# RWKV7 key norm as one reciprocal, third-order root steps, free PSUM in the order of work, both heads in 128 rows

## The chip, the cores and the metric

The kernel runs on one core of a Trainium2 chip. The metric is device time in microseconds (us), the median of several executions. Beside the times there is one profiled execution, whose trace is what all rows below come from.

## The reference

Two blocks run one after the other on 512 tokens of 2048 channels: a block with two attention layers, and a block that mixes an RWKV7 branch (16 heads of 64) with an HGRN2 branch (8 heads of 128). The change lies in the second block. What matters of the RWKV7 branch:

```python
kk = _heads(k * k_k, RWKV_HEAD)
kk = kk / jnp.maximum(jnp.sqrt(jnp.sum(kk * kk, -1, keepdims=True)), 1e-12)
k = k * (1.0 + (a - 1.0) * k_a)
o = _rwkv7_scan(rh, _heads(decay, RWKV_HEAD), kh, vh, -kk, kk * ah)
...
sa = jnp.einsum('bhij,bhj->bhi', S, a_t)
S = S * w_t[:, :, None, :] + sa[..., None] * b_t[:, :, None, :] + v_t[..., None] * k_t[:, :, None, :]
```

The normed key enters the state only as the pair `a_t = -kk` and `b_t = kk * a`, and only their product counts. The output of each head is then normed over its 64 channels, by the inverse root of a variance. The HGRN2 branch norms its heads in the same way.

## The kernel before

All large products are tiled as 128x128 weights by 512 tokens. Weights come from HBM in pieces of 128x512, are split into a high and a low part in fp32r (ScalarE writes `wh`, GpSimd writes `wl`), and each product is made of three matmuls: high by high, high by low, low by high. In the trace these are the `proj` matmuls.

The program runs the layers in order: the two attention layers, then the eight RWKV units (two heads each, so 128 channels), then the eight HGRN units, then the output product and a layer norm. Each unit has four column blocks of 48 `proj` matmuls (`mix_groups`). The rest of a unit's work is cut into steps that belong to threads: `rwkv_unit` makes the threads `prep` (decay, key norm, operands), `M` (pair matrices, triangular inverse, the recurrence over four chunks, the head norm), `K` and `B`.

The order of all instructions is fixed while the program is built. A `Clock` (L30) keeps a modelled time of each engine and of each tile. Between two triples of `proj` matmuls, `stream` calls `side` (L341), which goes through the threads and issues each thread's next step if `ready` (L337) says that the modelled results of the step before it, and the events it needs, lie in the past. A step that is needed before something else can go on is issued by `require` (L327), ready or not. Each engine then executes its own instructions strictly in that order, so that a step whose data or PSUM buffer is late holds up whatever stands behind it on the engine.

PSUM is held as four tags: `proj` with three buffers, `s` with two, `t` with two, `y` with one. `ps` (L227) takes the next buffer of a tag. In the modelled time the first write to it then waits until the buffer's last reader is done, but `ready` does not ask for that.

Steps that the change touches: `p_kk2` and `p_kk3` (L1318, L1325) sum the squares of the key per head and norm the key `kq`, with an inverse root by Ln and Exp on ScalarE and one Newton step (`newton_rsqrt`, L478) on VectorE; `m_ar` (L1395) scales the normed key, with a sign, by the decay; `m_split`, `m_split2` and `m_step` (L1402 to L1428) make, chunk by chunk, high and low parts of the operands `bk` and `ar` and from them the pair matrices, in two `s` buffers, one for each head; `small_rsqrt` (L487) is the inverse root of 128x8 or 128x4 numbers on VectorE, from an integer guess and three Newton steps, in `f_2` (L1671) and `fin2` (L1990). Other steps that the prediction names: `p_tok` (L1380) transposes an operand through a `t` buffer, `inv_8` (L1476) is 14 small VectorE instructions, `block_u` and `ch_u` (L1589, L1596) are the recurrence, `m_zo` (L1446) follows `m_step`, and `f_3` transposes the normed heads.

Nearly all instructions stand under one line in the trace, L175, the helper through which they are issued; they are told apart by their tiles.

Of the kernel before, what the change touches and what calls it, by code (L numbers as in the profile page):

```python
# [6 lines left out]
F32 = mybir.dt.float32  # L7
F32R = mybir.dt.float32r
U32 = mybir.dt.uint32
I32 = mybir.dt.int32  # L10
AF = mybir.ActivationFunctionType
ALU = mybir.AluOpType
# [17 lines left out]
class Clock:  # L30
# [7 lines left out]
    def __init__(self):  # L38
        self.t = dict.fromkeys(("tensor", "vector", "scalar", "gpsimd", "sync"), 0.0)
        self.w, self.r, self.free, self.dead = {}, {}, {}, set()  # L40
        self.fin = 0.0
        self.aset = None
        self.mode = None

        self.port = {"vector": [], "gpsimd": []}
# [11 lines left out]
    def note(self, eng, cost, outs, ins, lat=0.0, mode=None, shared=False):  # L57
        t = self.t[eng]
        lat += self.LAT[eng]
        use = {}  # L60
        for aps, kind in ((ins, 0), (outs, 1)):
            for ap in aps:
                name = ap.tensor.name
                assert name not in self.dead, name
                t = max(t, self.free.get(name, 0.0) if kind else 0.0)
                for c in self.cells(ap):
                    use[c] = max(kind, use.get(c, 0))
        for c, kind in use.items():
            f, e = self.w.get(c, (0.0, eng))
            if e != eng or eng != "tensor":  # L70
                t = max(t, f + self.HOP)
            if kind:
                f, e = self.r.get(c, (0.0, eng))
                t = max(t, f + self.HOP if e != eng else 0.0)
        if mode:
            if self.mode not in (None, mode):
                t += self.SWITCH
            self.mode = mode
        if shared:
            for s, f in self.port["gpsimd" if eng == "vector" else "vector"]:  # L80
                if s <= t < f:
                    t = f
            p = self.port[eng]
            p.append((t, t + cost))
            del p[:-24]
        self.t[eng] = t + cost
        fin = t + cost + lat
        for c, kind in use.items():
            d = self.w if kind else self.r
            if d.get(c, (0.0, eng))[0] <= fin:  # L90
                d[c] = (fin, eng)
        self.fin = max(self.fin, fin)

    def last(self, name):

        return max([v[0] for d in (self.w, self.r) for k, v in d.items() if k[0] == name] + [0.0])


def isap(x):
# [89 lines left out]
class Timed:  # L189
    def __init__(self, clock, nc):  # L190
        for n in ("tensor", "vector", "scalar", "gpsimd", "sync"):
            setattr(self, n, Engine(clock, getattr(nc, n), n))


class Kern:
# [29 lines left out]
    P = tmp  # L225
# [58 lines left out]
    def mm(self, out, lhsT, rhs, start, stop, **kw):  # L284
        self.nc.tensor.matmul(out, lhsT, rhs, start=start, stop=stop, **kw)
# [19 lines left out]
    def set(self, ev):  # L305
        self.ev[ev] = self.clock.fin
# [29 lines left out]

    def ready(self, th):  # L337
        return th["steps"] and th["ready"] <= self.clk and all(
            self.ev.get(e, 1e9) <= self.clk for e in th["steps"][0][1])

    def side(self):  # L341
        t0 = self.clk
# [126 lines left out]
        self.thread([(lambda: None, [("acc", layer)], None), (a,), (b, [], ("rsb", layer))],  # L469
                    carry=True)  # L470

    def rsqrt(self, m, r):

        nc = self.nc
        nc.scalar.activation(r, m, AF.Ln, scale=2.0 ** 16)
        nc.scalar.activation(r, r, AF.Exp, scale=-0.5, bias=self.l2c)

    def newton_rsqrt(self, r, m, t):  # L478

        nc = self.nc  # L480
        nc.vector.tensor_tensor(out=t, in0=r, in1=r, op=ALU.mult)
        nc.vector.scalar_tensor_tensor(out=t, in0=t, scalar=-0.5, in1=m, op0=ALU.mult,
                                       op1=ALU.mult)
        nc.vector.scalar_tensor_tensor(out=r, in0=t, scalar=1.5, in1=r, op0=ALU.add,
                                       op1=ALU.mult)

    def small_rsqrt(self, r, m, t):  # L487

        nc = self.nc
        nc.vector.tensor_scalar(r.bitcast(U32), m.bitcast(U32), 1, None, ALU.logical_shift_right)  # L490
        nc.vector.tensor_scalar(r.bitcast(I32), r.bitcast(I32), -1.0, float(0x5f3759df), ALU.mult,
                                ALU.add)
        for _ in range(3):
            self.newton_rsqrt(r, m, t)

    def silu_gate(self, ps, sg):

# [58 lines left out]
    def start(self):  # L556
        nc, I, const = self.nc, self.I, self.const
# [24 lines left out]
        load_x(1)  # L582
        self.ones = self.tile(self.cp, (128, 128), F32, "ones")
        nc.vector.memset(self.ones, 1.0)
        self.l2c = self.tile(self.cp, (128, 1), F32, "l2c")
        nc.vector.memset(self.l2c, 8.0 * float(np.log(2.0)))
        self.rsb = self.tile(self.cp, (128, T), F32, "rsb")
        self.load_raw(2)
        load_x(2)
# [669 lines left out]
    def rwkv_unit(self, st, u):  # L1259
        nc = self.nc  # L1260
        mm, mm3, tr, ps, P = self.mm, self.mm3, self.tr, self.ps, self.P
        c2 = {k: (v[:, u:u + 1]) for k, v in self.c2.items() if k not in ("mu", "omu")}
        S = {}
        sgt, kt, ly, mat = self.sgt, self.kt, self.ly, self.mat[u % 2]
        c4 = lambda t: t.rearrange("p (c t) -> p c t", c=4)
# [52 lines left out]
        def p_kk2():  # L1318
            p = head_sum(S["hi"], S["lo"])
            S["m"], S["rn"] = P("pm", (128, 516)), P("pr", (128, 516))  # L1320
            m, rn = S["m"][:, 0:512], S["rn"][:, 0:512]
            nc.vector.tensor_scalar(m, p, 1e-24, None, ALU.max)
            self.rsqrt(m, rn)

        def p_kk3():  # L1325
            m, rn = S["m"][:, 0:512], S["rn"][:, 0:512]
            self.newton_rsqrt(rn, m, S["sq"])
            nc.gpsimd.tensor_tensor(out=S["kq"], in0=S["kq"], in1=rn, op=ALU.mult)

        def p_dec():  # L1330
            S["cs"] = cs = P("pm", (128, 4, 129))
# [61 lines left out]
        own = [slice(0, 64), slice(64, 128)]  # L1393

        def m_ar():  # L1395
            S["ar"] = ar = P(f"ar{u % 2}", (128, 4, 2, 128))
            nc.vector.scalar_tensor_tensor(out=ar[:, :, 0, :], in0=c4(S["kq"]), scalar=-1.0,
                                           in1=S["P"][:, :, 0:128], op0=ALU.mult, op1=ALU.mult)
            nc.vector.tensor_tensor(out=ar[:, :, 1, :], in0=c4(st["r", u]),
                                    in1=S["P"][:, :, 1:129], op=ALU.mult)  # L1400

        def m_split(c):  # L1402
            def f():
                if c == 0:
                    S["zo"] = P("zo", (128, 4, 2, 128), bufs=2)
                bk = S["bk"][:, c]
                S["bkh", c] = x = P("bkhl", (128, 2, 2, 128), F32R, 2)
                S["arh", c] = y = P("arhl", (128, 3, 2, 128), F32R, 2)
                for h in range(2):
                    nc.scalar.activation(x[own[h], h], bk[own[h]], AF.Copy)  # L1410
                nc.scalar.activation(y[:, 2], S["ar"][:, c], AF.Copy)
            return f

        def m_split2(c):
            def f():
                ar, bk, x, y = S["ar"][:, c], S["bk"][:, c], S["bkh", c], S["arh", c]
                for h in range(2):
                    a, b = own[h], own[1 - h]
                    nc.scalar.activation(y[b, h], ar[a], AF.Copy)
                    nc.vector.tensor_tensor(out=x[b, h], in0=bk[a], in1=x[a, h].bitcast(F32),  # L1420
                                            op=ALU.subtract)
                    nc.vector.tensor_tensor(out=y[a, h], in0=ar[a], in1=y[a, 2].bitcast(F32),
                                            op=ALU.subtract)
            return f

        def m_step(c):  # L1428
            def f():
                p = [ps("s", (128, 2, 256)) for h in range(2)]  # L1430
                x = S["bkh", c]
                y = [S["arh", c][:, i].rearrange("p a t -> p (a t)") for i in range(3)]
                for i in range(2):
                    for h in range(2):
                        mm(p[h][:, i, :], x[own[h], h, i, :], y[2][own[h], :], i == 0, False,
                           skip_group_check=True)
                for h in range(2):
                    for i in range(2):
                        mm(p[h][:, i, :], x[:, h, i, :], y[h], False, i == 1, skip_group_check=True)
                for h in range(2):  # L1440
                    nc.vector.copy_predicated(out=kt[:, h, :], mask=self.mmask, data=p[h][:, 1, :])
                    nc.vector.copy_predicated(out=mat[:, 2 * c + h, :], mask=self.mmask,
                                              data=p[h][:, 0, :])
            return f
# [196 lines left out]
        def ch_o(c):  # L1641
# [17 lines left out]
            out=o.rearrange("p (c h) -> p c h", h=2), in_=v8(i), axis=mybir.AxisListType.X,  # L1659
            op=ALU.add)  # L1660
# [682 lines left out]
```

## Time and profile before

| what | value |
|---|---|
| three runs, us | 3031.47, 3031.53, 3036.08 |
| median, us | 3031.53 |
| profiled execution, time, us | 3026.69 |
| its span from first to last instruction, us | 3024.9 |
| TensorE busy | 2942.7 us, 97% of the span |
| VectorE, ScalarE, GpSimd busy | 52%, 43%, 45% |
| mean granted TensorE clock | 0.985 |

A busy TensorE is not one at its peak: matmuls overlap, and their ends are modelled. A granted clock of 1.00 is 2.4 GHz, one of 0.50 is 1.2 GHz.

### The profile page before, as it was taken

The numbers are of one execution on the slowest core, as the hardware profiler recorded it, in microseconds if no ns is written. First come the engines' busy times: TensorE is split into PE (matmuls) and PEld (weight loads), VectorE is DVE, ScalarE is ACT, GpSimd is POOL, SyncE is SP. The second block draws the span as 40 slices with busy tenths as digits, with TensorE's granted clock in tenths as the row PEclk, the third lists the DMA queues.
The fourth block names the chain that finished last, engine by engine and source line by source line (L and its number), as shares of the span: only waits on it lengthen the run. The fifth ranks groups of instructions, "written<-read, shape, count | busy, mean of one in ns | idle before, by whom it ended". The sixth has DMA issues, their size and how long they took to land. (4 is left out here: it accounts for less than half of the span.)

```text
span 3024.9 us, 47964 instructions
## 1 busy us (share of the span) xinstructions
PE 2942.7 (97%) x17904; PEld 2356.2 (78%) x17904; DVE 1560.2 (52%) x3481; ACT 1302.4 (43%) x2571; POOL 1351.4 (45%) x1105
## 2 busy tenths in 40 slices
PE   8999999999999999999999999999999999999996
PEld 5788888888888888888888876677677787888785
DVE  6433333343431235555531277767777766766436
ACT  6444444444433344444443364444444445545233
POOL 3444444444446543444445652223333344444575
PEclk9999999999999999999999999999989999999998
DMA  4333333333335432222234422222222222222343
GB/s 139 108 87 88 94 91 88 94 91 89 93 91 161 140 94 77 75 79 79 76 121 145 123 81 71 62 65 62 64 69 66 76 68 73 81 77 77 103 120 107
DMA packets 192088, 275.79 MB, mean 91 GB/s; under 512 B 50576, under 2 KB 65872, under 8 KB 191856
## 3 DMA queue, kind: packets, MB, share of 16 engines
q1 hardware_dynamic: 191856, 272.73, 31.6%
q8 instruction: 141, 2.31, 0.3%
q14 instruction: 91, 0.75, 0.1%
HBM read 254.51 MB, written 18.16 MB: 90 GB/s over the span
## 5 line engine op out<-in xcount | busy, mean ns | idle before, releaser
L175 POOL TENSOR_TENSOR wl<-raw,wh 128x512 fp32r<-128x512 f32 x847 | 1123.2, 1328 | 1606.8 <-ACT wh L175 1552.6
L175 PE MATMUL proj<-hh,wh 128*128 128x512 f32 x2624 | 1073.2, 409 | 7.1 <-ACT hh L175 5.9
L175 PE MATMUL proj<-hl,wh 128*128 128x512 f32 x2624 | 1036.7, 395 | 4.5 <-DVE hl L175 4.4
L175 PE MATMUL proj<-hh,wl 128*128 128x512 f32 x2624 | 1037.2, 395 | 3.2 <-POOL wl L175 3.1
L175 ACT ACTIVATE wh<-raw 128x512 fp32r<-128x512 f32 x848 | 530.7, 627 | 822.0 <-PE proj L175 587.1
L175 PEld LDWEIGHTS proj<-hh,wh 128*128 128x128 f32 x2624 | 498.8, 190 | 116.1 <-issue 10.6
L175 PEld LDWEIGHTS proj<-hh,wl 128*128 128x128 f32 x2624 | 499.1, 190 | 114.7 <-POOL wl L175 6.5
L175 PEld LDWEIGHTS proj<-hl,wh 128*128 128x128 f32 x2624 | 500.1, 191 | 95.7 <-DVE hl L175 8.0
L175 PE MATMUL proj<-yh,wh 128*128 128x512 f32 (+1 forms) x640 | 249.8, 390 | 0.0
L175 PE MATMUL proj<-yh,wl 128*128 128x512 f32 (+1 forms) x640 | 248.2, 388 | 0.7 <-POOL wl L175 0.4
L175 ACT ACTIVATE t<-t,sm 128x257 f32<-128x257 f32 (+5 forms) x256 | 133.0, 521 | 257.2 <-DVE sm L175 197.3
L175 PE MATMUL proj<-yl,wh 128*128 128x512 f32 (+1 forms) x632 | 240.9, 388 | 0.0
L175 PEld LDWEIGHTS proj<-yh,wl 128*128 128x128 f32 x640 | 120.2, 188 | 26.8 <-POOL wl L175 2.4
L175 DVE TENSOR_TENSOR pt<-proj,t 128x512 f32<-128x512 f32 x32 | 22.1, 691 | 229.1 <-PE proj L175 116.5
L175 PEld LDWEIGHTS proj<-yh,wh 128*128 128x128 f32 x640 | 120.3, 188 | 24.4 <-issue 0.9
L175 PEld LDWEIGHTS proj<-yl,wh 128*128 128x128 f32 x632 | 118.8, 188 | 23.9 <-issue 0.2
L175 DVE TENSOR_TENSOR qf<-proj,rsb 128x512 f32<-128x512 f32 x48 | 33.2, 691 | 154.5 <-PE proj L175 154.2
L175 DVE TENSOR_SCALAR t<-t,sm 128x256 f32<-128x256 f32 (+3 forms) x256 | 101.7, 418 | 6.7
L175 DVE COPY pt<-t 128x384 f32<-128x384 f32 (+1 forms) x96 | 51.2, 534 | 99.8 <-PE t L175 99.8
L175 DVE RECIPROCAL sm<-sm 128x1 f32<-128x1 f32 (+1 forms) x192 | 31.4, 164 | 117.4 <-ACT t L175 115.8
L175 PE MATMUL t<-ident,t 128*128 128x128 f32 x544 | 90.5, 272 | 0.0
L175 DVE CUSTOM_DVE_ANT_0 t<-s,c 128x128 f32<-128x128 f32 (+2 forms) x128 | 49.9, 390 | 71.6 <-PE s L175 71.6
(412 smaller groups left out, 3752.4 us busy)
## 6 DMA issues: line engine op xcount, KB each, us to landing
raw<-in_w_mix_dram SPq DMA_DIRECT2D x260, 256.0 KB, 3.0
raw<-in_w_fox_dram SPq DMA_DIRECT2D x256, 256.0 KB, 3.0
raw<-in_w_swa_dram SPq DMA_DIRECT2D x144, 256.0 KB, 3.0
raw<-in_w_foxo_dram SPq DMA_DIRECT2D x64, 256.0 KB, 3.2
raw<-in_w_swao_dram SPq DMA_DIRECT2D x64, 256.0 KB, 3.1
raw<-in_w_mixo_dram SPq DMA_DIRECT2D x64, 256.0 KB, 3.1
c<-cd SPq DMA_DIRECT2D x32, 256.0 KB, 3.7
xd<-pt SPq DMA_DIRECT2D x32, 256.0 KB, 2.4
```

The costliest lines, as they stand in the source:

```text
L175: r = f(*a, **k)
```

## The change

There are four edits, all in the second block's part of the program or in the order of its steps.

The key stays as it is, and the key that is taken out (`nk`, a new tile) is the key times the reciprocal of its squared norm: ScalarE's Exp gives the reciprocal at once, one Newton step for a reciprocal takes two VectorE instructions in place of three, and `m_ar`'s first instruction has two operands and no sign.

`small_rsqrt` has one third-order step and one Newton step after the guess, 9 instructions in place of 11.

`ready` asks in addition whether the PSUM buffers that the step takes are free in the modelled time (`banks`, for the steps named in `BANKS`, all of them of the second block).

The high and low parts of `bk` and `ar` keep both heads in 128 rows: two ScalarE and two VectorE instructions of 128 rows for each chunk in place of five and four (three of them of 128 rows). `m_step` then makes twelve matmuls of 64 rows (high by high, high by low, low by high, for two operands and two heads) in place of four of 64 rows and four of 128.

```diff
+BANKS = dict(p_lora="ss", m_step="ss", lev64="s", lev_m="s", **dict.fromkeys(
+    ("p_kk2", "p_bonus", "p_tok", "m_zo", "lev16", "lev16b", "lev32", "lev32b", "ch_z", "ch_u",
+     "ch_u2", "ch_u3", "ch_s", "f_3", "tok", "state", "fin3"), "t"))
 def ready(self, th):
         return th["steps"] and th["ready"] <= self.clk and all(
-            self.ev.get(e, 1e9) <= self.clk for e in th["steps"][0][1])
+            self.ev.get(e, 1e9) <= self.clk for e in th["steps"][0][1]) and self.banks(
+                th["steps"][0][0]) <= self.clk
+    def banks(self, f):
+        name = [n for n in f.__qualname__.split(".") if n not in ("<locals>", "f")][-1]
+        t = 0.0
+        for i, p in enumerate(BANKS.get(name, "")):
+            pool, bufs = self.psum[p]
+            q = self.slots.get((id(pool), p), [])
+            if i >= bufs - len(q):
+                t = max(t, self.clock.last(q[i - (bufs - len(q))]) + self.clock.HOP)
+        return t
...
-    def rsqrt(self, m, r):
+    def rsqrt(self, m, r, n=1):
-        nc.scalar.activation(r, r, AF.Exp, scale=-0.5, bias=self.l2c)
+        nc.scalar.activation(r, r, AF.Exp, scale=-0.5 * n, bias=self.l2c[:, n - 1:n])
...
 def small_rsqrt(self, r, m, t):
-        for _ in range(3):
-            self.newton_rsqrt(r, m, t)
+        nc.vector.tensor_tensor(out=t, in0=r, in1=r, op=ALU.mult)
+        nc.vector.tensor_tensor(out=t, in0=t, in1=m, op=ALU.mult)
+        nc.vector.scalar_tensor_tensor(out=t, in0=t, scalar=-10.0 / 3, in1=t, op0=ALU.add,
+                                       op1=ALU.mult)
+        nc.vector.scalar_tensor_tensor(out=r, in0=t, scalar=5.0, in1=r, op0=ALU.add, op1=ALU.mult)
+        self.newton_rsqrt(r, m, t, 0.375)
...
 def p_kk3():
-            self.newton_rsqrt(rn, m, S["sq"])
-            nc.gpsimd.tensor_tensor(out=S["kq"], in0=S["kq"], in1=rn, op=ALU.mult)
+            nc.vector.tensor_tensor(out=m, in0=m, in1=rn, op=ALU.mult)
+            nc.vector.scalar_tensor_tensor(out=rn, in0=m, scalar=-2.0, in1=rn, op0=ALU.add,
+                                           op1=ALU.mult)
+            S["nk"] = P("nk")
+            nc.gpsimd.tensor_tensor(out=S["nk"], in0=S["kq"], in1=rn, op=ALU.mult)
...
 def m_ar():
-            nc.vector.scalar_tensor_tensor(out=ar[:, :, 0, :], in0=c4(S["kq"]), scalar=-1.0,
-                                           in1=S["P"][:, :, 0:128], op0=ALU.mult, op1=ALU.mult)
+            nc.vector.tensor_tensor(out=ar[:, :, 0, :], in0=c4(S["nk"]), in1=S["P"][:, :, 0:128],
+                                    op=ALU.mult)
...
 def m_split(c):
-                S["bkh", c] = x = P("bkhl", (128, 2, 2, 128), F32R, 2)
-                S["arh", c] = y = P("arhl", (128, 3, 2, 128), F32R, 2)
-                for h in range(2):
-                    nc.scalar.activation(x[own[h], h], bk[own[h]], AF.Copy)
-                nc.scalar.activation(y[:, 2], S["ar"][:, c], AF.Copy)
+                S["x", c] = x = P("bkhl", (128, 2, 2, 128), F32R, 2)
+                S["y", c] = y = P("arhl", (128, 2, 2, 128), F32R, 2)
+                nc.scalar.activation(x[:, 0], S["bk"][:, c], AF.Copy)
+                nc.scalar.activation(y[:, 0], S["ar"][:, c], AF.Copy)
...
 def m_split2(c):
-                for h in range(2):
-                    a, b = own[h], own[1 - h]
-                    nc.scalar.activation(y[b, h], ar[a], AF.Copy)
-                    nc.vector.tensor_tensor(out=x[b, h], in0=bk[a], in1=x[a, h].bitcast(F32),
+                for t, hl in ((S["bk"], S["x", c]), (S["ar"], S["y", c])):
+                    nc.vector.tensor_tensor(out=hl[:, 1], in0=t[:, c], in1=hl[:, 0].bitcast(F32),
                                             op=ALU.subtract)
-                    nc.vector.tensor_tensor(out=y[a, h], in0=ar[a], in1=y[a, 2].bitcast(F32),
-                                            op=ALU.subtract)
...
 def m_step(c):
-                for i in range(2):
-                    for h in range(2):
-                        mm(p[h][:, i, :], x[own[h], h, i, :], y[2][own[h], :], i == 0, False,
-                           skip_group_check=True)
-                for h in range(2):
+                for n, (a, b) in enumerate(((0, 0), (0, 1), (1, 0))):
                     for i in range(2):
-                        mm(p[h][:, i, :], x[:, h, i, :], y[h], False, i == 1, skip_group_check=True)
+                        for h in range(2):
+                            mm(p[h][:, i, :], x[own[h], a, i, :], y[own[h], b, :],
+                               n == i == 0, n == 2 and i == 1, skip_group_check=True)
```

The clock also keeps, in `used`, the last modelled use of each tile, which `last` now returns; the value is the same as before.

## Rows read from the trace of the kernel before

**Rows 1.** Windows: busy of each engine, granted clock; RWKV stage, then HGRN stage.

```profile
core 0: us, PE busy (x) PEld busy (x) DVE busy (x) ACT busy (x) POOL busy (x), PEclk, DMA share, GB/s
1778.00:2405.00 627.00, 587.82 (x4913) 445.71 (x4914) 477.46 (x1016) 276.73 (x540) 200.81 (x153) 0.94 0.26 68
2405.00:2880.00 475.00, 471.74 (x3579) 379.24 (x3576) 299.75 (x591) 216.73 (x417) 225.76 (x183) 1.00 0.27 79
```

**Rows 2.** Waits of PE in 1778:2405: for whom, us in total, times, longest.

```profile
PE t L175 <- DVE pm L175: 11.1, 4, 2.8
PE t L175 <- DVE chz L175: 5.1, 5, 1.0
PE t L175 <- DVE em L175: 4.2, 2, 2.1
PE t L175 <- ACT tokk L175: 3.7, 1, 3.7
PE t L175 <- ACT zo L175: 2.9, 6, 0.5
...
PE s L175 <- DVE yh L175: 1.8, 2, 0.9
```

**Rows 3.** Timeline of PE around one DVE pm wait: start, us, matmul, idle before.

```profile
2207.07 0.66 PE L175 MATMUL t<-ident,bk 128*128 128x128 f32 x4
2210.49 0.69 PE L175 MATMUL t<-chz,wd 64*64 64x64 f32 x4 [2.77 <-DVE pm L175]
```

**Rows 4.** Timeline of DVE in that stretch: chz, first of 14 inv_8 instructions, pm.

```profile
2206.72 0.29 DVE L175 TENSOR_TENSOR chz<-t,zo 128x128 f32<-128x128 f32 x1 [0.92 <-PE t L175]
2206.93 0.16 DVE L175 TENSOR_TENSOR invt<-ly 64x14 f32<-64x14 f32 x1
...
2209.76 0.68 DVE L175 TENSOR_SCALAR pm<-t 128x512 f32<-128x512 f32 x1
```

**Rows 5.** Windows, columns as Rows 1, after waits; first two: ends of four.

```profile
1964.30:1974.40 10.10, 9.67 (x29) 6.98 (x30) 7.13 (x14) 2.64 (x5) 4.48 (x3) 0.50 0.09 27
...
2298.80:2305.50 6.70, 6.70 (x19) 4.88 (x19) 6.27 (x12) 1.34 (x3) 1.37 (x1) 0.50 0.16 42
...
2240.80:2250.90 10.10, 9.34 (x112) 7.81 (x113) 6.54 (x15) 1.99 (x5) 1.26 (x1) 0.50 0.20 54
...
2184.70:2188.50 3.80, 3.39 (x39) 2.65 (x39) 1.96 (x8) 1.81 (x5) 0.00 (x0) 1.00 0.23 69
```

**Rows 6.** Timeline of PE where the clock comes back: two slow starts, two fast.

```profile
2216.09 0.63 PE L175 MATMUL proj<-hl,wh 128*128 128x512 f32 x1
2216.51 0.56 PE L175 MATMUL proj<-hh,wl 128*128 128x512 f32 x1
...
2217.14 0.39 PE L175 MATMUL proj<-hl,wh 128*128 128x512 f32 x1
2217.37 0.39 PE L175 MATMUL proj<-hh,wl 128*128 128x512 f32 x1
```

**Rows 7.** Timeline of DVE, f_2's chain in one unit, up to its last instruction.

```profile
2148.96 0.37 DVE L175 SCALAR_TENSOR_TENSOR gn<-gn 128x8 f32<-128x8 f32 x2
...
2152.00 1.13 DVE L175 TENSOR_TENSOR gn<-gn 128x8 f32<-128x8 f32 x1
...
2154.59 0.69 DVE L175 TENSOR_TENSOR zo<-zo,gn 128x512 f32<-128x512 f32 x1
```

**Rows 8.** Timeline of DVE: last subtractions of a chunk, ahead of a chz wait.

```profile
2182.88 0.42 DVE L175 TENSOR_TENSOR bkhl<-bk,bkhl 64x256 fp32r<-64x256 f32 x1
2183.32 1.42 DVE L175 TENSOR_TENSOR arhl<-ar,arhl 64x256 fp32r<-64x256 f32 x1
2184.77 0.29 DVE L175 TENSOR_TENSOR chz<-t,zo 128x128 f32<-128x128 f32 x1
```

**Rows 9.** Timeline of PE: one m_step, eight matmuls of both forms, and what follows.

```profile
2186.47 1.17 PE L175 MATMUL s<-arhl,bkhl 64*128 64x256 f32 x8
2187.48 0.40 PE L175 MATMUL proj<-hh,wh 128*128 128x512 f32 x1
```

More of the change, by code (lines that the diff above doesn't have):

```diff
@@ L40, in __init__ @@
         self.w, self.r, self.free, self.dead = {}, {}, {}, set()
+        self.used = {}
         self.fin = 0.0
@@ L87, in note @@
         fin = t + cost + lat
+        for name in {c[0] for c in use}:
+            self.used[name] = max(fin, self.used.get(name, 0.0))
         for c, kind in use.items():
@@ L94, in last @@
     def last(self, name):
-        return max([v[0] for d in (self.w, self.r) for k, v in d.items() if k[0] == name] + [0.0])
+        return self.used.get(name, 0.0)
 def isap(x):
@@ L470, in norm_scale, with newton_rsqrt @@
                     carry=True)
-    def rsqrt(self, m, r):
+    def rsqrt(self, m, r, n=1):
         nc = self.nc
         nc.scalar.activation(r, m, AF.Ln, scale=2.0 ** 16)
-        nc.scalar.activation(r, r, AF.Exp, scale=-0.5, bias=self.l2c)
-    def newton_rsqrt(self, r, m, t):
+        nc.scalar.activation(r, r, AF.Exp, scale=-0.5 * n, bias=self.l2c[:, n - 1:n])
+    def newton_rsqrt(self, r, m, t, f=1.0):
         nc = self.nc
         nc.vector.tensor_tensor(out=t, in0=r, in1=r, op=ALU.mult)
-        nc.vector.scalar_tensor_tensor(out=t, in0=t, scalar=-0.5, in1=m, op0=ALU.mult,
+        nc.vector.scalar_tensor_tensor(out=t, in0=t, scalar=-0.5 * f ** 3, in1=m, op0=ALU.mult,
                                        op1=ALU.mult)
-        nc.vector.scalar_tensor_tensor(out=r, in0=t, scalar=1.5, in1=r, op0=ALU.add,
+        nc.vector.scalar_tensor_tensor(out=r, in0=t, scalar=1.5 * f, in1=r, op0=ALU.add,
                                        op1=ALU.mult)
@@ L584, in start @@
         nc.vector.memset(self.ones, 1.0)
-        self.l2c = self.tile(self.cp, (128, 1), F32, "l2c")
-        nc.vector.memset(self.l2c, 8.0 * float(np.log(2.0)))
+        self.l2c = self.tile(self.cp, (128, 2), F32, "l2c")
+        for i in range(2):
+            nc.vector.memset(self.l2c[:, i:i + 1], 8.0 * (i + 1) * float(np.log(2.0)))
         self.rsb = self.tile(self.cp, (128, T), F32, "rsb")
@@ L1322, in p_kk2 @@
             nc.vector.tensor_scalar(m, p, 1e-24, None, ALU.max)
-            self.rsqrt(m, rn)
+            self.rsqrt(m, rn, 2)
         def p_kk3():
             m, rn = S["m"][:, 0:512], S["rn"][:, 0:512]
-            self.newton_rsqrt(rn, m, S["sq"])
-            nc.gpsimd.tensor_tensor(out=S["kq"], in0=S["kq"], in1=rn, op=ALU.mult)
+            nc.vector.tensor_tensor(out=m, in0=m, in1=rn, op=ALU.mult)
[3 more added lines that the diff above has]
+            nc.gpsimd.tensor_tensor(out=S["nk"], in0=S["kq"], in1=rn, op=ALU.mult)
         def p_dec():
@@ L1405, in f @@
                     S["zo"] = P("zo", (128, 4, 2, 128), bufs=2)
-                bk = S["bk"][:, c]
-                S["bkh", c] = x = P("bkhl", (128, 2, 2, 128), F32R, 2)
-                S["arh", c] = y = P("arhl", (128, 3, 2, 128), F32R, 2)
-                for h in range(2):
-                    nc.scalar.activation(x[own[h], h], bk[own[h]], AF.Copy)
-                nc.scalar.activation(y[:, 2], S["ar"][:, c], AF.Copy)
+                S["x", c] = x = P("bkhl", (128, 2, 2, 128), F32R, 2)
+                S["y", c] = y = P("arhl", (128, 2, 2, 128), F32R, 2)
+                nc.scalar.activation(x[:, 0], S["bk"][:, c], AF.Copy)
+                nc.scalar.activation(y[:, 0], S["ar"][:, c], AF.Copy)
             return f
@@ L1415, in f @@
             def f():
-                ar, bk, x, y = S["ar"][:, c], S["bk"][:, c], S["bkh", c], S["arh", c]
-                for h in range(2):
-                    a, b = own[h], own[1 - h]
-                    nc.scalar.activation(y[b, h], ar[a], AF.Copy)
-                    nc.vector.tensor_tensor(out=x[b, h], in0=bk[a], in1=x[a, h].bitcast(F32),
-                                            op=ALU.subtract)
-                    nc.vector.tensor_tensor(out=y[a, h], in0=ar[a], in1=y[a, 2].bitcast(F32),
+                for t, hl in ((S["bk"], S["x", c]), (S["ar"], S["y", c])):
+                    nc.vector.tensor_tensor(out=hl[:, 1], in0=t[:, c], in1=hl[:, 0].bitcast(F32),
                                             op=ALU.subtract)
@@ L1430, in f @@
                 p = [ps("s", (128, 2, 256)) for h in range(2)]
-                x = S["bkh", c]
-                y = [S["arh", c][:, i].rearrange("p a t -> p (a t)") for i in range(3)]
-                for i in range(2):
-                    for h in range(2):
-                        mm(p[h][:, i, :], x[own[h], h, i, :], y[2][own[h], :], i == 0, False,
-                           skip_group_check=True)
-                for h in range(2):
+                x = S["x", c]
+                y = S["y", c].rearrange("p n a t -> p n (a t)")
+                for n, (a, b) in enumerate(((0, 0), (0, 1), (1, 0))):
                     for i in range(2):
-                        mm(p[h][:, i, :], x[:, h, i, :], y[h], False, i == 1, skip_group_check=True)
+                        for h in range(2):
+                            mm(p[h][:, i, :], x[own[h], a, i, :], y[own[h], b, :],
+                               n == i == 0, n == 2 and i == 1, skip_group_check=True)
                 for h in range(2):
```

## The prediction

> **What bounds the kernel now.** I read the windows by stage first. The RWKV stage is 627.0 us long and TensorE is busy for 587.8 of it at a mean clock of 0.94; the HGRN stage is 475.0 us with 471.7 busy at 1.00 [rows 1]. The attention layers run before 1778 us, and no edit reaches their instructions. So TensorE sets the end in both stages of the second block, and only the RWKV stage has something to give back: 627.0 - 587.8 = 39 us of idle, and about 0.06 x 627 = 38 us for the clock. VectorE is busy for 477 us there, 76%: it is not the bound on average, but it is the engine that is late when TensorE waits.
>
> Next the waits of TensorE in that stage [rows 2]. The reader should sort them by what was late. **Buffers:** four waits, 11.1 us in all, that end with `pm`, and one of 3.7 us that ends with `tokk`, 14.8 us together. The timeline of one shows the kind: the transposes of `bk` start at 2207.07, and the next matmul, `chz` by `wd`, starts at 2210.49 after 2.77 us of idle [rows 3]. Its operand `chz` was written from 2206.72 to 2207.01. What it lacked was a `t` buffer: `p_kk2` had filled it, and VectorE's read of it, `pm`, runs only at 2209.76, behind the 14 instructions of `inv_8` that begin at 2206.93 [rows 4]. That is exactly what `ready` does not ask for. The six waits for `zo` (2.9 us) and the two of `s` for `yh` (1.8 us) are buffers too [rows 2]: `m_zo` and `m_step` fill the only free ones. **Data:** the waits for `chz` (5.1 us in five) and `em` (4.2 us in two) end with VectorE's results, not with a buffer; with `em` it is `f_2`'s last instruction just ahead of it, at 2154.59 [rows 7], on which `f_3`'s transposes wait.
>
> Last the clock. After each of four of the five long buffer waits the granted clock is 0.50, for 10.1, 10.1, 6.7 and 6.7 us, 33.6 us in all; after one `em` wait it is 0.50 for 10.1 us; after a `chz` wait of 1.0 us it stays at 1.00 [rows 5]. At 1.2 GHz two `proj` matmuls start 0.42 us apart, at 2.4 GHz 0.23 [rows 6]. So a slow microsecond loses 1 - 0.23 / 0.42 = 0.45 us: 33.6 x 0.45 = 15.1 us behind the buffer waits, and 4.5 us behind the one for `em`.
>
> **The change part by part.** All gains are TensorE time of the RWKV stage, which sets the end, so a microsecond there is one of the whole.
>
> *Free PSUM looked at: the long waits.* The step that would wait is left, and `proj` triples go in its place; these are work that must be done anyway. The most it can spare is 14.8 us. The least: the modelled clock that decides is also the one that judged `chz` ready, and there the chip was 1.0 us late each time [rows 2], so 5 x 1.0 stays, and 9.8 is spared. I take 12, since the late engine is the same one in four of the five.
>
> *The clock behind them.* At most 15.1. A wait of 1.0 us has no slow window behind it [rows 5], so even the remnant would keep the clock; the least is half, 7.5, if other pauses fall into those stretches. I take 12.
>
> *The short buffer waits.* Between 0 and 2.9 + 1.8 = 4.7 us. I take 3.
>
> *Third-order root.* Two VectorE instructions fewer in `f_2`. One costs 0.37 / 2 = 0.18 us, or 1.13 when it is held up [rows 7]; so each of the two `em` waits of 2.1 shrinks by 0.4 to 2.1. With the clock behind it this is between 0.8 and 4.2 + 4.5 = 8.7 us. I take 4. In the HGRN stage the same edit lies beside a busy TensorE [rows 1] and gives nothing.
>
> *Both heads in 128 rows, VectorE's and ScalarE's side.* A chunk has two subtractions in place of four, of the same 256 columns, 0.42 us each when not held up, and in the row ahead of a `chz` wait one takes 1.42 [rows 8]. That one delays `chz` by the 1.0 us of the wait. With half as many subtractions I take half of 5.1, 2.5 us, between 0 and 5.1. ScalarE's three instructions fewer for each chunk and the one VectorE instruction fewer of the key norm (0.69, as the 128x512 instruction of [rows 7]) lie beside TensorE's work; they cost and give nothing unless that cover goes, in which case the eight units would get 8 x 0.69 = 6 us back at most. The new tile adds no wait: GpSimd does one multiplication as before, and `m_ar` waits for it as before.
>
> *Both heads in 128 rows, TensorE's side.* One `m_step` takes from 2186.47 to 2187.48, 1.01 us [rows 9]. Its four matmuls of 128 rows have 256 columns, half of a `proj` matmul's 0.23, so 4 x 0.115 = 0.46; the four of 64 rows, with the load and the changes of form, take the remaining 0.55. If two heads run side by side, a pair is 0.115, the fixed part is 0.55 - 2 x 0.115 = 0.32, and six pairs make 0.32 + 0.69 = 1.01: no change. If a pair costs half of that 0.55, six make 1.65, and 32 steps lose 32 x 0.64 = 20 us. If the fixed part went wholly, they would gain 10. I take 0: two heads of 64 rows are already issued in turn in the first half of this step, and 0.55 for four leaves no room for running one by one with full loads.
>
> The Trainium skill (TensorE: Matmul & The Clock Gate, LDWEIGHTS) says that a weight load's time goes with its columns and not with its rows, and gives columns / 1.2 in ns, so 0.107 us for 128. By that rule alone the change has twelve full loads for eight, and the sum would be an estimated 32 x 4 x 0.107 = 14 us worse. The same skill (TensorEngine Tiling (Array Packing), Key Properties) lets different tiles load in parallel, by which nothing is lost; the 1.01 us of the row bears out neither alone.
>
> *What the new order costs.* Steps that went together are now split by `proj` triples. Each split is a change of form; the nearest price is the fixed part above, 0.32. With two more a unit, 16 x 0.32 = 5 us; none to twice as many gives 0 to 10.
>
> **The sum:** 12 + 12 + 3 + 4 + 2.5 + 0 - 5 = 28.5 us less. The profiled execution took 3026.7 us (a span of 3024.9 and 1.8 around it) and would take 2998.2. The median of the runs was 3031.5, 4.8 above it, and I carry the difference over: 3003.0 us. The next wait to be late is then the one for `chz`, with the plan's own error.
>
> **The rivals.** *The clock stays down* (0.15): the long waits shrink to 1 us but the tiny matmuls of the inverse, which stand in the slow window at 2240.8 with 112 matmuls [rows 5], keep it slow. Then 9.8 + 3 + 2.5 + 0.8 - 3 = 13 us are gained: 3018. Against it: the window after a 1.0 us wait has 39 matmuls, most of them small, at 1.00.
>
> *The pairs run one after another* (0.05): 28.5 - 20 = 8.5 gained, 3023. This is what the rule on loads points at, in a stronger form.
>
> *The gate changes nothing* (0.09): it works on modelled times, and if these take `pm` to be done when it isn't, the same waits stand in other places. That gives the small terms less the splits, 3 + 2.5 - 5, within a microsecond of no change: 3031. Against it: the other readiness test, on the same clock, misses by 1.0 us only.
>
> *The gate holds the recurrence back* (0.09, the slower side): with two `t` buffers, other threads take each one that comes free, and `ch_z` to `ch_s` and the steps behind them slip past the column blocks that supply `proj` work. Then the evacuation of the next unit's block calls for them with `require`, not asking for readiness, and TensorE stands as with `tokk`: 3.7 us, and 10.1 x 0.45 = 4.5 behind it, 8.2 a unit. From four of the eight units on, 4 x 8.2 = 33, this eats the 28.5 and decides; with six it is 49, 21 us slower: 3052. Against it: seven units of four blocks of 48 `proj` matmuls, 1344 by 0.23 us [rows 6], are 309 us, half of the stage, to put between.
>
> *Everything falls* (0.10): both ends of all terms, 14.8 + 15.1 + 4.7 + 8.7 + 5.1 = 48 and some of the 10 of `m_step`, 55: 2976.
>
> **How the numbers follow.** My forecast, 2988 to 3015, has 0.52. The range reaches to "everything falls" on one side and to "the gate changes nothing" on the other, 2972 to 3031, and leaves out the slower case and half of the unchanged one. A measurement of this kernel can tell about 0.2%, 6 us, from no change: faster means below 3025.5. Faster: 0.52 + 0.15 + 0.05 + 0.10 = 0.82; same 0.09; slower 0.09.
>
> **What would show it.** Right: the waits of TensorE in the RWKV stage show no `pm` or `tokk` wait over 1.2 us; the stage is some 28 us shorter with a mean clock of 0.97 or more; `m_step`'s twelve matmuls take 0.95 to 1.1 us from first start to the next step's; the subtractions are two a chunk at 0.42; nothing moves before 1778 us and under 3 us in the HGRN stage. Wrong: as many idle microseconds under other names; an `m_step` of 1.3 us or more; long waits at the start of a unit's column blocks with the clock at 0.50 behind them; or a stage as long as before with fewer waits, the time having gone into matmuls that start further apart.

## The result and the profile after

| | before | after |
|---|---|---|
| median, us | 3032.4 (4 runs) | 2997.8 (4 runs) |
| lowest and highest, us | 3031.5, 3036.1 | 2995.7, 3005.3 |
| profiled execution, us | 3026.7 | 2995.7 |

The ratio is 0.9888 (95% interval 0.9869 to 0.9908): 34.6 us between the medians, or 1.1%, faster. The forecast was 3003.0, 28.5 us less than before.

The page's first part of the kernel after (busy time, share of the span, instructions), and then two windows of it, RWKV stage and HGRN stage, with the columns of [rows 1]:

```profile
PE 2924.0 (98%) x18032; PEld 2347.8 (78%) x18032; DVE 1512.6 (51%) x3378; ACT 1258.1 (42%) x2473; POOL 1352.4 (45%) x1105
```

```profile
1771.00:2374.00 603.00, 575.46 (x5095) 442.63 (x5094) 437.20 (x940) 238.33 (x455) 202.36 (x153) 0.97 0.26 72
2374.00:2850.00 476.00, 472.84 (x3552) 380.37 (x3552) 298.07 (x572) 215.71 (x416) 228.53 (x186) 1.00 0.25 79
```

The RWKV stage has 27.5 us without TensorE in place of 39, and a clock of 0.97 in place of 0.94; VectorE does 437 us of work there in place of 477. The HGRN stage is as long as before. That is where the time was expected to come from.

The waits of TensorE in the RWKV stage after (for whom, us in total, times, longest):

```profile
PE t L178 <- DVE zo L178: 12.4, 6, 3.2
PE proj L178 <- ACT wh L178: 3.5, 2, 3.0
PE proj L178 <- POOL wl L178: 3.5, 3, 1.8
PE t L178 <- DVE sbd L178: 1.7, 1, 1.7
...
PE t L178 <- ACT zo L178: 1.0, 2, 0.5
PE t L178 <- DVE chz L178: 0.7, 1, 0.7
...
PE t L178 <- DVE pm L178: 0.2, 1, 0.2
```

Of the buffer waits of [rows 2], `pm` fell from 11.1 us to 0.2, `tokk` from 3.7 to none, `zo` by ScalarE from 2.9 to 1.0. The data wait for `chz` fell from 5.1 to 0.7. But a wait that was 4.2 us before (there named `em`) is now the largest: six times the transposes of `f_3` wait for VectorE's `zo`, 12.4 us. One of them, first on TensorE, then on VectorE:

```profile
2268.08 0.39 PE L178 MATMUL proj<-hh,wl 128*128 128x512 f32 x1
2271.66 1.08 PE L178 MATMUL t<-ident,zo 128*128 128x128 f32 x4 [3.20 <-DVE zo L178]
...
2272.97 0.63 PE L178 MATMUL proj<-hl,wh 128*128 128x512 f32 x1
2273.40 0.63 PE L178 MATMUL proj<-hh,wl 128*128 128x512 f32 x1
```

```profile
2261.62 1.57 DVE L178 TENSOR_TENSOR invt<-ly 64x256 f32<-64x256 f32 x1
...
2263.68 0.60 DVE L178 TENSOR_TENSOR invt<-ly 64x256 f32<-64x256 f32 x1
...
2265.88 1.18 DVE L178 TENSOR_TENSOR invt<-ly,x 64x256 f32<-64x256 f32 x1
...
2267.44 0.67 DVE L178 TENSOR_REDUCE gn<-zo 128x8 f32<-128x512 f32 x1
2268.14 1.25 DVE L178 TENSOR_SCALAR gn<-gn 128x8 f32<-128x8 f32 x3
...
2270.83 0.69 DVE L178 TENSOR_TENSOR zo<-zo,gn 128x512 f32<-128x512 f32 x1
```

`f_2` (the `gn` instructions) starts at 2267.44 because VectorE was still busy with `inv_16`, whose multiplications take 0.60 to 1.57 us in these rows where the plan takes 0.34. From there `f_2` takes 4.1 us. TensorE stands for 3.2 us, and afterwards its matmuls start 0.43 us apart, at 1.2 GHz.

Not all six are of this kind. `inv_16` stands ahead of `f_2` in two of them, this one and the one that ends at 2045.57. In the one that ends at 2208.86 it is `f_2` itself that is long, 8.4 us from its first to its last instruction; the last alone takes 1.64 us where the row above has 0.69:

```profile
2200.27 0.69 DVE L178 TENSOR_REDUCE gn<-zo 128x8 f32<-128x512 f32 x1 [0.70 <-ACT zo L178]
...
2207.07 1.64 DVE L178 TENSOR_TENSOR zo<-zo,gn 128x512 f32<-128x512 f32 x1
```

The third reading is one `m_step` after, with the next two `proj` matmuls:

```profile
2158.47 0.98 PE L178 MATMUL s<-arhl,bkhl 64*128 64x256 f32 x12
2159.38 0.50 PE L178 MATMUL proj<-hh,wh 128*128 128x512 f32 x1
2159.72 0.40 PE L178 MATMUL proj<-hl,wh 128*128 128x512 f32 x1
```

Twelve matmuls of 64 rows take 0.91 us up to the next start, and that next matmul takes 0.34 to its successor in place of 0.23, so 1.25 together. Before it was 1.01 [rows 9] and 0.23, 1.24 together; the second `proj` matmul after the step of [rows 9] is

```profile
2187.71 0.40 PE L175 MATMUL proj<-hl,wh 128*128 128x512 f32 x1
```

In the trace the two matmuls of a pair start 0.004 us apart or less, and from the second pair on the next one starts 0.12 us later: the two of a pair run side by side. The 0.1 us of the change of form has moved from the middle of the step (there the first matmul of 128 rows takes 0.22 us to the next one, the others 0.12) to its end. Where `t<-chu,yh`, of 64 rows too, follows the step, it took 1.26 us before (four times) and takes 0.91 after.

### The profile page after: what moved, and what is told of

Its sections match the earlier page's. It is cut to its first block, busy times and chain, and to the rows that moved or that the text cites. A ratio compares the mean times of both kernels' runs of the same rounds, so it can differ in the third digit from the quotient of the medians.

```text
span 2993.9 us, 48010 instructions
## 1 busy us (share of the span) xinstructions
PE 2924.0 (98%) x18032; PEld 2347.8 (78%) x18032; DVE 1512.6 (51%) x3378; ACT 1258.1 (42%) x2473; POOL 1352.4 (45%) x1105
## 4 chain that ended last, share of the span: by engine, by line
PE 88%; DVE 8%; DMA 2%; issue 1%; ACT 1%; POOL 0%; SPq 0%; DVEq 0%; POOLq 0%; ACTq 0%
PE proj L178 71%; PE t L178 7%; PE s L178 6%; PE y L178 3%; DVE gn L178 1%; DVE invt L178 1%; DVE hh L178 1%; DVE pm L178 1%; DVE ly L178 1%; DMA raw<-in_w_fox_dram 0%; DVE zo L178 0%; DVE pr L178 0%; SPq L178 0%; DMA raw<-in_w_mix_dram 0%; DVE raw L178 0%
## 5 line engine op out<-in xcount | busy, mean ns | idle before, releaser
L178 DVE RECIPROCAL sm<-sm 128x1 f32<-128x1 f32 (+1 forms) x192 | 31.4, 164 | 117.8 <-ACT t L178 116.3
```

Source lines behind the costliest of these rows:

```text
L178: r = f(*a, **k)
```

## The experiments

Each number is a median; the ratio is to runs of the kernel before beside it (interval in brackets). The table also reads each profiled execution in the same way: over the stretch that begins with the 6401st `proj` matmul and ends with the 10001st (the same 3600 in every kernel), "idle" is its length less TensorE's busy time, and VectorE's work is its busy time; "clock" is (1 - mean granted clock) x span of the whole execution, the time that a clock always at 2.4 GHz would have spared if all of it went by the clock. The mean clock has three decimals, so "clock" is good to some 1.5 us. The last three columns are of one execution each, which can lie off its kernel's median: by 2 us below for the kernel after, 4 below for the gate alone, 10 above for the kernel before at margin 0.15.

| kernel | median, us | ratio | idle | clock | VectorE |
|---|---|---|---|---|---|
| before | 3032.4 | 1 | 42.8 | 45.4 | 835 |
| after | 2997.8 | 0.9888 (0.9869 to 0.9908) | 30.7 | 32.9 | 788 |
| gate alone | 3012.4 | 0.9948 (0.9929 to 0.9967) | 31.2 | 33.1 | 825 |
| after without gate | 3001.5 | 0.9905 (0.9891 to 0.9920) | 28.0 | 42.0 | 780 |
| 128 rows alone | 3008.6 | 0.9927 (0.9911 to 0.9944) | 35.0 | 42.1 | 792 |
| root alone | 3022.3 | 0.9966 (0.9953 to 0.9979) | 37.5 | 48.3 | 824 |
| before, margin 0.15 | 3042.4 | 1.0046 (1.0030 to 1.0063) | 47.6 | 70.2 | 838 |
| after, margin 0.15 | 2989.1 | 0.9869 (0.9846 to 0.9892) | 20.6 | 35.9 | 779 |
| 128 rows alone, four subtractions | 3031.2 | 1.0006 (0.9996 to 1.0015) | 45.9 | 48.5 | 825 |
| after, f_3 held | 2997.4 | 0.9896 (0.9881 to 0.9911) | 26.5 | 38.9 | 784 |
| after, inv_16 priced | 2998.6 | 0.9889 (0.9871 to 0.9907) | 22.6 | 51.0 | 777 |
| the same, margin 0.15 | 2981.9 | 0.9842 (0.9827 to 0.9857) | 18.8 | 29.8 | 778 |
| after, key norm as before | 2997.1 | 0.9885 (0.9865 to 0.9905) | 21.7 | 44.9 | 794 |
| after, four subtractions | 3001.6 | 0.9905 (0.9890 to 0.9920) | 31.4 | 36.0 | 818 |

### The gate alone, and all but the gate

```diff
+BANKS = dict(...)
 def ready(self, th):
...
-            self.ev.get(e, 1e9) <= self.clk for e in th["steps"][0][1])
+            self.ev.get(e, 1e9) <= self.clk for e in th["steps"][0][1]) and self.banks(
+                th["steps"][0][0]) <= self.clk
```

> The kernel before with the gate on free PSUM alone. My theory (waits for PSUM buffers and the slow clock behind them): 27 us less than before (12 + 12 + 3), less about 5 for split steps, so 3005 to 3012, with no wait for pm or tokk over 1.2 us. Rival one (the relief of VectorE is what counts): under 8 us less, 3024 or more. Rival two (any new order of steps moves the time as much): no particular value, and the waits that go come back under other names.

The reverse takes these lines out of the changed kernel.

> The changed kernel without the gate: key norm, root steps and both heads in 128 rows stay. My theory: 4 to 7 us less than before, 3025 to 3028, with the long waits for pm still there. Rival one (VectorE's relief): 25 us or more less, 3007 or below. Rival two: anything, but the gains of this run and of the gate alone don't add up to that of the whole change.

Measured: the gate alone takes 3012.4, just past the slow end of 3005 to 3012, and gives 17.7 us against the 3030.1 of the kernel before beside it; everything but the gate gives 28.6. The stretch of before, of the gate alone and of the whole change, in one window each (columns as [rows 1]):

```profile
1730.51:2951.66 1221.15, 1178.36 (x9011) 921.77 (x9010) 834.98 (x1670) 545.46 (x1040) 511.83 (x398) 0.97 0.28 76
```

```profile
1731.45:2932.97 1201.52, 1170.28 (x9011) 911.34 (x9010) 824.77 (x1670) 541.75 (x1038) 508.37 (x398) 0.98 0.29 78
```

```profile
1730.53:2920.71 1190.18, 1159.48 (x9140) 914.25 (x9138) 788.29 (x1566) 500.80 (x942) 512.18 (x398) 0.98 0.27 78
```

With the gate alone the same 9011 matmuls need 19.6 us less. Idle falls by 11.6, where the sum had 15 (12 for the long waits, 3 for the short ones), and the clock's part by 12.3, where it had 12; by difference some 4 us come back as work. These are hardly the split steps: in the stretch TensorE comes back to `proj` from other matmuls 290 times before and 300 times with the gate, and the `proj` matmul after such a return takes 0.34 us to the next in place of 0.23, so the ten make 1 us. The rest is open, and the rounded clock can hold part of it. No `pm` or `tokk` wait over 0.5 us is left:

```profile
PE t L175 <- DVE zo L175: 4.9, 7, 1.9
PE t L175 <- DVE chu L175: 3.6, 5, 1.4
PE proj L175 <- POOL wl L175: 2.9, 4, 0.8
...
PE t L175 <- DVE pm L175: 0.5, 2, 0.2
```

So the long waits went, and the clock behind them came back, as was forecast of the gate; but the `pm` waits also go without it, as the next runs show, so their absence alone does not show that the gate did it. My theory said 4 to 7 us for the rest, and it gave 28.6, more than the rival of VectorE's relief asked for (25). On top of the rest the gate adds 3.7 us between medians, with intervals of the ratios that overlap (0.9869 to 0.9908, and 0.9891 to 0.9920). The gains don't add, 17.7 and 28.6 against 34.6. That fits edits that spare the same waits, and it was also the sign of rival two, of a mere new order; the 11.7 us that are missing are no more than order alone moves (below).

### Both heads in 128 rows alone, and with four subtractions

The first takes `m_split`, `m_split2` and `m_step` of the change, nothing else. In the kernel before, ScalarE's five instructions for a chunk are four of 64 rows and one of 128, and VectorE's four are all of 64 rows, where "The change" says that three have 128.

> The kernel before with both heads in 128 rows alone. My theory: 0 to 5 us less than before, since m_step costs TensorE the same (1.01 us before; 0.91 plus 0.10 at the next matmul after) and two subtractions fewer for each chunk spare part of the 5 us of chz waits. If the pairs ran one after another: 20 us more.

The second cuts its two subtractions again:

```diff
-                    nc.vector.tensor_tensor(out=hl[:, 1], in0=t[:, c], in1=hl[:, 0].bitcast(F32),
-                                            op=ALU.subtract)
+                    for h in range(2):
+                        nc.vector.tensor_tensor(out=hl[own[h], 1], in0=t[own[h], c],
+                                                in1=hl[own[h], 0].bitcast(F32), op=ALU.subtract)
```

> Both heads in 128 rows alone, but with each of VectorE's two subtractions of a chunk cut into two of 64 rows, so that VectorE has four a chunk as before (0.42 us each) while ScalarE and TensorE have the new work. If VectorE's relief is what made the 128-row edit worth 21 us, it is worth 5 or less here, 3025 or more. If TensorE's or ScalarE's side made it, it stays at 3012 or less. Between: shared.

Measured: 21.5 us less than the kernel before alone, four times the most that was expected, and nothing (1.0006) with four subtractions. The stretches of the two:

```profile
1730.13:2935.88 1205.75, 1170.79 (x9139) 920.06 (x9138) 791.57 (x1606) 502.59 (x944) 511.27 (x398) 0.97 0.28 77
```

```profile
1731.65:2955.22 1223.57, 1177.69 (x9139) 919.32 (x9138) 824.72 (x1670) 500.08 (x942) 510.36 (x398) 0.97 0.28 76
```

Both have the same 9139 matmuls and about the same of ScalarE (503 and 500 us, against 545 before); they differ by 33 us of VectorE, and by 18 us of length. ScalarE's relief and the new matmuls, without VectorE's relief, give nothing. The waits of the one with two, then of the one with four:

```profile
PE proj L175 <- ACT wh L175: 7.5, 4, 4.1
PE t L175 <- DVE zo L175: 6.4, 2, 3.5
...
PE t L175 <- DVE pm L175: 0.2, 1, 0.2
```

```profile
PE t L175 <- DVE em L175: 10.1, 3, 3.7
PE t L175 <- DVE chu L175: 8.3, 8, 1.4
...
PE t L175 <- DVE pm L175: 0.8, 1, 0.8
```

In neither are the `pm` waits of before. They went without a gate, as soon as the order of steps was another; with four subtractions other waits for VectorE took their place.

### The root alone, and the key norm taken back

The third-order `small_rsqrt` in the kernel before:

> The kernel before with the third-order root alone. My theory: 1 to 4 us less than before, from the two em waits; the rival that it does nothing on its own: within 2 us.

Measured: 7.8 us less (ratio 0.9966), twice the most expected. Its first waits:

```profile
PE t L175 <- DVE zo L175: 5.6, 4, 3.2
PE t L175 <- ACT tokk L175: 3.7, 1, 3.7
```

The waits of before that it was meant for are hardly shorter: of the four for `zo`, three are of `f_3`'s transposes, 3.8 us with one of 3.2, where before had the two for `em`, 4.2 us. The `pm` waits are gone here too, without any gate, while the one for `tokk` stays. I don't count this as evidence for the reason that I had given; it is a changed order.

The changed kernel with `p_kk2`, `p_kk3` and `m_ar` as before:

```diff
-            self.rsqrt(m, rn, 2)
+            self.rsqrt(m, rn, 1)
...
+            self.newton_rsqrt(rn, m, S["sq"])
+            nc.gpsimd.tensor_tensor(out=S["kq"], in0=S["kq"], in1=rn, op=ALU.mult)
```

> The changed kernel with the key norm as before: an inverse root with a Newton step of three VectorE instructions, and the normed key in both places. One 128x512 VectorE instruction a unit more, 0.69 us, eight in all. Theory of VectorE's relief, at the rate of the 128-row edit (about 30 us of VectorE spared for 21 us of time): 5.5 us of VectorE cost 3 to 5 us, 2999 to 3003. Theory that the key norm lies beside other work, as predicted: within 2 us of the changed kernel.

Measured: 2997.1 against 2997.8, no difference. The key norm on its own in the kernel before wasn't tried.

### How much is order

The plan's `MARGIN`, by which a step's readiness is put later, from 0.10 to 0.15 us, in the kernel before and in the changed one. The work is the same, in another order.

> The kernel before with the plan's margin of readiness at 0.15 us in place of 0.10, nothing else: the same work in a slightly other order. If the waits for pm belong to the way of ordering (my theory), they come back and the time stays within 6 us of before. If they belong to one unlucky order (rival: any new order helps), the time falls by 10 us or more, as with the root steps alone, where the pm waits were gone too.

> The changed kernel with the margin at 0.15 us: another order of the changed work. My theory: within 6 us of the changed kernel, 2992 to 3004. The rival of the lucky order: 10 us or more above it, 3008 or more.

Measured: the kernel before gets slower by 0.46%, 13.6 us; the changed one is faster by 8.7 us between medians, more than the 6 expected, though the intervals of its two ratios overlap (0.9869 to 0.9908, and 0.9846 to 0.9892). So order alone moved the kernel before by 14 us, and a single edit's number above, the gate's 17.7 too, can hold that much of chance. That the change as a whole gains doesn't hang on it, but how much does: at 0.15 it is worth 2989.1 / 3042.4 = 0.9825, at 0.10 0.9888. What I expected of the `pm` waits was wrong: they did not come back in the kernel before at 0.15. The first lines of its waits:

```profile
PE proj L175 <- ACT wh L175: 7.1, 2, 3.6
PE y L175 <- DVE chu L175: 5.2, 3, 2.5
PE t L175 <- DVE chz L175: 4.4, 5, 1.0
```

The rival that any new order helps is refuted as well, since this one costs. The names of the waits belong to an order; the idle time does so less, 42.8 and 47.6 us for the kernel before at the two margins, 30.7 and 20.6 for the changed one.

### After: holding f_3, and pricing inv_16

```diff
+        if f.__name__ == "f_2":
+            th["ready"] += 3.0
         th["fin"] = fin
```

> The changed kernel with the transposes after the head norm (f_3) held back by 3 us in the plan. They are what TensorE waits for most now (12.4 us in six waits, each ending with VectorE's last instruction of f_2). My theory: these waits vanish and with them part of the slow clock behind three of them, 12 to 18 us less than the changed kernel, about 2983. Rival: the transposes are called for by another step before they are ready, and the waits stay, within 4 us of the changed kernel.

Measured: 2997.4, no gain, although the six `zo` waits are gone from the list, which now begins

```profile
PE proj L178 <- POOL wl L178: 5.7, 6, 1.8
PE t L178 <- DVE ev L178: 3.7, 2, 2.6
PE proj L178 <- ACT wh L178: 3.5, 3, 1.9
PE t L178 <- DVE chz L178: 3.3, 3, 1.6
```

The time is the rival's, the way to it is neither's: idle fell by only 4 us of the 12.4, and the clock's part rose by 6. The next experiments go to the plan's error itself: the four multiplications of `inv_16` get 0.3 us more in the plan.

```diff
+            far = 0.3 if m == "tensor_tensor" and len(out.ap) == 4 and out.partition_size() == 64 and n == 256 else 0.0
-            return 0.075 + n / (1920.0 if one else 960.0) + 0.06 * bool(points) + 2 * acc
+            return far + 0.075 + n / (1920.0 if one else 960.0) + 0.06 * bool(points) + 2 * acc
```

> The changed kernel with one duration of the plan mended: the four 64x256 multiplications of inv_16, for which the plan takes 0.34 us, are given 0.3 us more, as the chip shows (0.61 to 0.65 when not held up). My theory: what is left of TensorE's waits comes from VectorE being later on the chip than in the plan; with the plan nearer, steps are put later and the waits fall by a third, 8 to 14 us less than the changed kernel, about 2987. Rival: VectorE is simply the engine in short supply in the stage, and another estimate only moves the waits (as holding f_3 back did): within 4 us of the changed kernel.

> The same with the plan's margin at 0.15 us, which alone took the changed kernel to 2989. My theory: the gains add, 2975 to 2984. Rival, as above: 2985 to 2995.

Measured: 2998.6 with the price alone, no gain, as the rival had it; 2981.9 with the margin at 0.15 as well, 7 us below the margin alone (with intervals that overlap) and the shortest time of all, 0.9842 of before. That lies in the range for gains that add, but the price alone had none to add. In the profiled execution of the first, idle fell by 8 us, a quarter and not the third of the theory, 30.7 to 22.6, but the clock's part rose by 18, from 32.9 to 51.0. By the median clock of all runs, 0.986 against 0.988 for the kernel after, it rose by some 6. With the margin both are low, 18.8 and 29.8. The theory is supported for the direction of the waits and did not foresee the clock.

The two kernels here differ by the margin alone and were measured side by side: 16.7 us between them are again order. Holding `f_3` and the price, on the other hand, are new orders that moved the changed kernel by less than 1 us between medians.

### After with four subtractions

The cut of the subtractions, as above, in the changed kernel.

> The changed kernel with each of VectorE's two subtractions of a chunk cut into two of 64 rows. If VectorE's relief and the gate work on the same waits, this loses less than the 22 us that it lost without the gate: 5 to 15 us above the changed kernel, 3003 to 3013. If they work on different waits, the full 20 us: 3018 or more.

Measured: 3001.6, 3.8 us above the changed kernel between medians and 5 by the ratios, whose intervals overlap: the low end of the 5 to 15 of waits in common, and far from the full 20. With the gate in place, 30 us more of VectorE (818 against 788) cost much less than the 22.6 us that 33 us of VectorE cost without it. My explanation, argued and not shown by a run of its own: the gate lets TensorE pass the steps for which VectorE is late, so VectorE's lateness costs less; the relief makes it less late, so the gate has less to pass.

Whether all this is only order can be asked of the table. Sort its kernels by the gate and by the two subtractions of 128 rows. With neither, four orders (before, root alone, before at 0.15, 128 rows with four subtractions) have ratios of 0.9966 to 1.0046. With one of the two, whatever else they have, four kernels (gate alone, after without gate, 128 rows alone, after with four subtractions) have 0.9905 to 0.9948. With both, the other six have 0.9842 to 0.9896. No order in one group reaches the next, though at both borders the groups are closer than the intervals are wide. The means are 1.000, 0.992 and 0.988: the first of the two edits gives some two thirds of the gain, the second the rest.

## Why the prediction was right, and where it wasn't

**The total** was right: 28.5 us forecast, 34.6 measured, and both stages as said: the RWKV stage shorter at a better clock, the HGRN stage unchanged to 1 us, and the 6401st `proj` matmul, shortly before the RWKV stage, at 1730.5 us in both. The size is in part luck. One term was far too small and the terms were added as if they met different waits, and the two errors nearly cancel. Over the stretch of 3600 `proj` matmuls the whole change gives 31.0 us: idle falls by 12.1, where the sum had 17.5 without the root (12 + 3 + 2.5), the clock's part by 12.5, where it had 12, and TensorE's work falls by some 6 beyond the clock, where 5 were to be lost.

**The gate's terms** for the waits (12 and 3) and for the clock (12) were near for the gate alone, where 11.6 and 12.3 were read, each in one execution. The 5 lost to splits were too much: a change of form costs about 0.1 us, not the 0.32 of the working, and TensorE returns to `proj` 282 times in the changed kernel against 290 before. The step that failed is the sum: I added the other edits to it as if they met other waits.

**Both heads in 128 rows, VectorE's side** was mis-sized: 2.5 us, taken from the five `chz` waits; alone it is worth 21.5. I looked only at the waits that stand just behind a subtraction. A VectorE that has some 40 us less to do is less late everywhere. The cut into four subtractions takes the whole gain away with TensorE's and ScalarE's part left as it is, so VectorE's part is what made it, as far as the 22.6 us exceed what order moves. The sentence that VectorE is "the engine that is late when TensorE waits" already held it; I gave it no price.

**Third-order root**: 4 us for shorter `em` waits. Alone it measured 7.8, but with hardly shorter waits of that kind (3.8 us against 4.2), and after the whole change they are 12.4 us in place of 4.2. The mechanism is not borne out: two instructions fewer matter less than when VectorE comes to `f_2` and how long its instructions are held up there. The size lies in the range, but order alone moves more than that.

**TensorE's side of the 128 rows, and the key norm**, at nothing each, were right: 1.25 us against 1.24 for `m_step` and its successor, and 2997.1 against 2997.8 without the new key norm. The sign of 0.95 to 1.1 us for the step alone was missed by a little, with 0.91, since part of its cost went to the successor. By the Trainium skill's rule a weight load goes by its columns (TensorE: Matmul & The Clock Gate, LDWEIGHTS); the estimated 14 us that I drew from it counted twelve loads one after another, and 1.25 against 1.24 us leaves no room for that. In the trace the two loads of a pair start 0.003 us apart, at 2158.468 and 2158.471 in the step shown, so six pairs stand where two pairs and four single loads stood. The trace agrees with the Trainium skill (TensorEngine Tiling (Array Packing), Key Properties), that different tiles load and multiply in parallel.

**The rivals.** "The gate holds the recurrence back" is refuted by the gate alone, and so is "the gate changes nothing", as far as its 17.7 us exceed what order moves. "The pairs run one after another" is refuted by the 1.25 us. "The clock stays down" was partly there: the granted clock is 0.50 for about 3 us after three of the six `f_3` waits, and with `inv_16` priced it cost back what idle had gained. The rival that I had not listed is the one that bears on the shares: the edits in part replace each other, and order alone moves anything from nothing to 17 us.

**Still open:** how much of the gate's 17.7, of the 21.5 and of the 7.8 us is order. The margin measures the size of it, not its part in a given edit.

## What to carry to other kernels

Where one engine's lateness makes the bottleneck wait, a plan that passes late steps and less work on the late engine can cure the same waits; price them together, and not one by one from the waits that stand behind an instruction. Before a single edit's number is believed in a kernel whose order is planned, move a parameter of the plan that changes no work, and see how far the time goes. Read idle and clock together: an edit can take a quarter off the first and lose it to the second.

## What the runs showed of the hardware

One program's executions differ in the granted clock, and the time goes with it. The nine runs of the root alone are 3010.5 and 3012.1 us at a mean clock of 0.990, and 3019.1 to 3023.9 at 0.983 to 0.985. That is some 11 us for 0.006, about 2 us for each 0.001, where 3.0 would be the most (0.001 x 3020 us, if all work went by the clock). So a gain under 10 us needs many runs of both kernels.

A VectorE multiplication of 64x256 takes 0.60 us in `inv_16` when it runs freely (2263.68 above) and 1.57 (2261.62) when GpSimd's `wl` is under way; it ends at 2263.19, 0.45 us after this `wl`:

```profile
2261.40 1.34 POOL L178 TENSOR_TENSOR wl<-raw,wh 128x512 fp32r<-128x512 f32 x1
```

The Trainium skill (GPSIMD Engine Reference, Specifications) has the two engines share their SBUF interfaces, with contention for VectorE instructions that have two SBUF inputs; the rows agree, with 0.97 us more here.
